# Attention of a hybrid encoder block: softmax weights and values in high and low parts, and the row maximum as a minimum of negated scores

## The chip, the cores and the metric

One core of one Trainium2 chip runs the whole block as one program. The metric is device time in microseconds (us) from the first to the last instruction of one execution, with what lies around it; lower is better. A step of 0.5% is about 7.5 us here.

## The reference, cut to what matters

The block normalizes 512 tokens of width 1024, projects them once, runs a gated mixing branch (A) and a dilated window attention (B) side by side, projects their sum back, and then does a product-key expert retrieval that takes most of the time. The change touches only branch B, whose three dilated windows the kernel merges into one masked softmax: the mask holds the logarithm of how many windows contain a pair of tokens.

```
    s = jnp.einsum('nbqhd,nbkhd->nbhqk', qb, kw).astype(jnp.float32) * (HEAD_DIM ** -0.5)
    ...
    m = jnp.max(s, axis=-1, keepdims=True)
    p = jnp.exp(s - m)
    l = jnp.sum(p, axis=-1)
    o = jnp.einsum('nbhqk,nbkhd->nbqhd', p, vw.astype(jnp.float32))
    l_t = jnp.swapaxes(l, 2, 3)
    o = o / l_t[..., None]
```

There are 8 heads of 64 columns and 4 blocks of 128 query tokens, so 32 pairs of block and head.

## The kernel before, in words

The order of instructions on each engine is the order in which they are written (a manual schedule): each engine works through its own list, and semaphores that the tile framework places hold an instruction until its operands are there and its output buffer is free. In the code T is TensorE, V is VectorE (DVE), S is ScalarE (ACT), G is GpSimd (POOL), Q is SyncE's DMA queue.

Most large products are done in two parts. `split` (lines 78 to 80) copies a float32 tensor into an fp32r tile (the high part, on ACT) and subtracts that from the source (the low part, on DVE by `sub`); a product is then three passes, high by high, high by low and low by high. The attention's second product, weights by values, is not done so before the change: it is a plain float32 product, and the trace counts two TensorE instructions for each.

The attention runs over s = 0 to 31, with i the block of queries and h the head. Its parts are staged in a loop (lines 493 to 504), which writes for each s, in this order: the exponential of s+2 (ACT, line 409), the transposes of s+1 (four on PE, line 416) and their copy out of PSUM (ACT, line 418), the scores of s+3 (two products of 512 columns on PE, lines 394 and 395), the masked maximum of s+3 (DVE, line 402) with its negation (line 404), and the product with the values of s (PE, line 429, in `att_mix`). Once in eight steps `att_out` divides a block by the sums (DVE), `att_sq` squares it (ACT), and `turn_gated` transposes a part of branch A (PE, ACT and DVE, lines 487 to 491).

Buffers: the score tiles in PSUM are two ("pu"), the transposed weights in PSUM are one ("tr"), the softmax tiles `sm` two (tag w1), their transposes `st` two (tag w2). Ahead of the loop the scores and maxima of 0, 1 and 2 are done, the exponentials of 0 and 1, the transposes of 0, and the four value tiles `vs` (lines 479 to 483), which are evicted from the projection's PSUM tiles by ACT and DVE in turn. Behind the loop comes the output projection (line 237), of which the first products need nothing of the attention.

`h2T` is a pair of tiles of 128 x 8 x 512 that hold the second layer's input later on; until then `h2T[1]` holds low parts of the keys.

Of the kernel before, what the change touches and what calls it, by code (L numbers as in the profile page):

```python
# [8 lines left out]
F32 = mybir.dt.float32  # L9
F32R = mybir.dt.float32r  # L10
# [4 lines left out]
AF = mybir.ActivationFunctionType  # L15
ALU = mybir.AluOpType
# [4 lines left out]
NB = 4  # L21
# [4 lines left out]
HD = 64  # L26
# [18 lines left out]
def peer_block(ctx: ExitStack, tc: tile.TileContext, A, out):  # L45
    nc = tc.nc
    V, S, G, T, Q = nc.vector, nc.scalar, nc.gpsimd, nc.tensor, nc.sync
# [9 lines left out]
    tk = tr_ctx.enter_context(tc.tile_pool(name="tk", bufs=1))  # L57
# [20 lines left out]
    def split(hi, lo, src, sub):  # L78
        S.copy(hi, src)  # L79
        sub.tensor_tensor(lo, src, hi.bitcast(F32), op=ALU.subtract)  # L80
# [48 lines left out]
    def inv_root(pool, ss, n, cols=1, name="sd", bias=eps):  # L129

        sd = pool.tile([128, 2, cols], F32, name=name, bufs=4 if name == "sd" else 1)
        S.activation(sd[:, 0, :], ss, AF.Sqrt, bias=bias, scale=1.0 / n)
        V.reciprocal(sd[:, 1, :], sd[:, 0, :])
        return sd[:, 1, :]
# [107 lines left out]
    def drain(gen, n=10 ** 6):  # L242
        for _ in range(n):
            if next(gen, True):
                return


    h2T = [keep.tile([128, KT, 512], F32R, name=f"h2T{i}") for i in range(2)]
    qk = {"q": [], "k": []}

# [39 lines left out]
    ps = []  # L290
# [19 lines left out]
    xrs = inv_root(tk, xss, 1024, NB, name="xrs")  # L310
# [3 lines left out]
    ps = []  # L314
# [17 lines left out]
    masks = {}  # L332
# [7 lines left out]
    ps = []  # L340
# [11 lines left out]
    va = tk.tile([128, NB, 512], F32, name="va")  # L352
# [7 lines left out]
    ps = []  # L360
# [22 lines left out]
    pss, sms, pos, sts = {}, {}, {}, {}  # L383
    l8 = tk.tile([128, NB, 2, H], F32, name="l8")
    mxs = {}

    def att_scores(s):
        if s < NS:
            i, h = divmod(s, H)
            if h == 0:  # L390
                mask_load(i + 1)
            pss[s] = pu.tile([128, 512], F32, name="pu")
            q, k, klo = qk["q"][h // 2][0][:, h % 2, i * 128:(i + 1) * 128], *qk["k"][h // 2]
            T.matmul(pss[s], q, k[:, h % 2, :], start=True, stop=False)
            T.matmul(pss[s], q, klo[:, h % 2, :], start=False, stop=True)

    def att_max(s):
        if s < NS:
            i, h = divmod(s, H)
            sms[s] = tk.tile([128, 512], F32, name="sm", tag="w1", bufs=2)  # L400
            mx = mxs[s] = tk.tile([128, 2], F32, name="mx", bufs=4)
            V.tensor_tensor_reduce(sms[s], pss.pop(s), masks[i], op0=ALU.add, op1=ALU.max, scale=HD ** -0.5,
                                   scalar=-3.0e38, accum_out=mx[:, 0:1])
            V.tensor_scalar(mx[:, 1:2], mx[:, 0:1], -1.0, None, op0=ALU.mult)

    def att_exp(s):
        if s < NS:
            i, h = divmod(s, H)
            S.activation(sms[s], sms[s], AF.Exp, bias=mxs.pop(s)[:, 1:2], accum_out=l8[:, i, 0, h:h + 1])

    def att_turn(s):
        if s < NS:
            sm = sms.pop(s)
            ps = pr.tile([128, 512], F32, name="tr")
            for j in range(NB):
                T.transpose(ps[:, j * 128:(j + 1) * 128], sm[:, j * 128:(j + 1) * 128], ident)  # L416
            sts[s] = tk.tile([128, 512], F32, name="st", tag="w2", bufs=2)
            S.copy(sts[s], ps)

    def att_mix(s):  # L420
        i, h = divmod(s, H)
        if h == 0:
            if i % 2:
                pos[i] = pr.tile([128, 512], F32, name="po")
            else:
                pos[i] = pr.tile([128, 512], F32, name="acc", bufs=4)
        st = sts.pop(s)
        for j in range(NB):
            T.matmul(pos[i][:, h * HD:(h + 1) * HD], st[:, j * 128:(j + 1) * 128], vs[:, j, h * HD:(h + 1) * HD],  # L429
                     start=(j == 0), stop=(j == NB - 1))  # L430

    msq = tk.tile([128, 2, NB], F32, name="msq")
    bo = {}
# [15 lines left out]
    ps = []  # L449
    gen = proj(16, hT, ps)  # L450
    drain(gen, 4)
    for g in range(0, 8, 2):
# [3 lines left out]
        for j in range(2):  # L456
            us = ua[:, :, (g + j) * 64:(g + j + 1) * 64]
            V.scalar_tensor_tensor(us, pm[:, j, :].rearrange("p (b c) -> p b c", b=NB), bsp[:, g + j:g + j + 1], us,
                                   op0=ALU.add, op1=ALU.mult)
        drain(gen, 1)  # L460
    for b in range(NB):
        sq = tk.tile([128, 512], F32, name="scr", tag="w3", bufs=2)
        sumsq(sq, ua[:, b, :], msq[:, 0, b:b + 1])
    att_scores(0)
    att_max(0)
    drain(gen, 2)
    urs = inv_root(tk, msq[:, 0, :], 512, NB)
    warm(AF.Exp)
    att_scores(1)
    att_max(1)  # L470
    drain(gen, 2)
    att_exp(0)
    for b in range(NB):
        V.tensor_scalar(ua[:, b, :], ua[:, b, :], urs[:, b:b + 1], None, op0=ALU.mult)
    drain(gen)
    vs = tk.tile([128, NB, 512], F32, name="vs", tag="va")
    att_exp(1)
    att_turn(0)
    for b in range(NB):
        if b % 2:  # L480
            V.tensor_scalar(vs[:, b, :], ps[b], xrs[:, b:b + 1], None, op0=ALU.mult)
        else:
            S.activation(vs[:, b, :], ps[b], AF.Copy, scale=xrs[:, b:b + 1])
    att_scores(2)
    att_max(2)

    def turn_gated(k):
# [5 lines left out]
    for s in range(NS):  # L493
        att_exp(s + 2)
        att_turn(s + 1)
        if s % H == 1 and s > H:
            att_sq(s // H - 1)
        att_scores(s + 3)
        att_max(s + 3)
        if s % H == 0 and s:  # L500
            att_out(s // H - 1)
        if s % H == 4:
            turn_gated(s // H)
        att_mix(s)
# [355 lines left out]
    for t8 in range(N8):  # L860
        a, c = hot.pop(0)
# [198 lines left out]
    for e in range(NK):  # L1060
# [16 lines left out]
        n = min(int(quota), 128 - dotted)  # L1077
# [110 lines left out]
```

## Time and profile before

| | before |
|---|---|
| median of 3 runs | 1513.45 us (1510.02 to 1516.0) |
| the profiled execution: time | 1517.74 us |
| the profiled execution: span of the trace | 1515.9 us |
| mean granted TensorE clock | 0.988 |
| PE busy, share of the span | 97% |
| DVE busy | 76% |
| ACT busy | 42% |
| POOL busy | 19% |

The profiled execution took 1.84 us more than its span, and 4.3 us more than the median of the runs. Busy shares are means over stages with different limits. The attention lies in about 60 us of the span, between 145 and 205 us.

### The profile page before, as it was taken

The numbers are of one execution on the slowest core, as the hardware profiler recorded it, in microseconds if no ns is written. First come the engines' busy times: TensorE is split into PE (matmuls) and PEld (weight loads), VectorE is DVE, ScalarE is ACT, GpSimd is POOL, SyncE is SP. The second block draws the span as 40 slices with busy tenths as digits, with TensorE's granted clock in tenths as the row PEclk, the third lists the DMA queues.
The fourth block names the chain that finished last, engine by engine and source line by source line (L and its number), as shares of the span: only waits on it lengthen the run. The fifth ranks groups of instructions, "written<-read, shape, count | busy, mean of one in ns | idle before, by whom it ended". The sixth has DMA issues, their size and how long they took to land.

```text
span 1515.9 us, 21652 instructions
## 1 busy us (share of the span) xinstructions
PE 1469.3 (97%) x7977; PEld 1302.9 (86%) x7977; DVE 1159.2 (76%) x2407; ACT 640.4 (42%) x1088; POOL 294.3 (19%) x230
## 2 busy tenths in 40 slices
PE   8899999999899999999999999999999999999997
PEld 6677988888888889789999999999999999987785
DVE  3644554789899967878888888888888888877775
ACT  5354753344455643434333333333333333333334
POOL 0242001444700000012221222222122222211002
PEclk9999999999999999999999999999999999999999
DMA  4231032333356775479999999889999999988764
GB/s 158 91 97 63 29 110 86 92 94 104 105 208 252 264 278 195 132 260 357 333 333 340 333 328 341 311 314 332 331 333 330 316 330 333 312 285 285 263 209 158
DMA packets 130073, 357.21 MB, mean 236 GB/s; under 512 B 9136, under 2 KB 62128, under 8 KB 113456
## 3 DMA queue, kind: packets, MB, share of 16 engines
q1 hardware_dynamic: 104624, 196.45, 39.5%
q0 software_dynamic: 18432, 134.23, 23.2%
q10 hardware_dynamic: 6912, 25.17, 4.1%
q8 instruction: 62, 1.02, 0.3%
q14 instruction: 43, 0.35, 0.1%
HBM read 325.40 MB, written 30.41 MB: 235 GB/s over the span
## 4 chain that ended last, share of the span: by engine, by line
PE 73%; DVE 13%; DMA 6%; issue 3%; ACT 3%; POOL 1%; ACTq 0%; SPq 0%; DVEq 0%; POOLq 0%
PE pu L187 31%; PE acc L990 27%; PE acc L237 7%; DMA vraw<-in_uv_dram 4%; DVE ohb L829 3%; DVE oha L833 2%; DVE ulo L167 2%; DMA uraw<-in_uT_dram 2%; DVE vlo L80 2%; PE tr L416 1%; ACT vhi L79 1%; PE tr L712 1%; PE pu L237 1%; PE po L429 1%; POOL ulo L167 1%
## 5 line engine op out<-in xcount | busy, mean ns | idle before, releaser
L187 PE MATMUL pu<-h2T,uhi 128*128 128x384 f32 (+2 forms) x2336 | 451.0, 343 | 3.1 <-ACT act L742 2.4
L187 PEld LDWEIGHTS pu<-h2T,uhi 128*128 128x128 f32 x2336 | 409.8, 189 | 18.9 <-ACT act L742 2.7
L936 POOL DMA_INDIRECT uv<-in_uv_dram,ei x128 | 168.1, 1313 | 847.5 <-DVE xlast L951 355.7
L80 DVE TENSOR_TENSOR vlo<-vraw,vhi 128x1024 fp32r<-128x1024 f32 x128 | 156.8, 1225 | 151.5 <-ACT vhi L79 151.5
L79 ACT CAST vhi<-vraw 128x1024 fp32r<-128x1024 f32 x128 | 134.5, 1051 | 282.0 <-issue 169.8
L990 PE MATMUL acc<-vlo,wahi 128*128 128x512 f32 x768 | 240.8, 395 | 7.8 <-DVE vlo L80 7.1
L990 PE MATMUL acc<-vhi,wahi 128*128 128x512 f32 x768 | 240.3, 394 | 2.3 <-ACT wahi L79 2.2
L990 PE MATMUL acc<-vhi,walo 128*128 128x512 f32 x768 | 239.3, 393 | 0.0
L187 PE MATMUL pu<-h2T,ulo 128*128 128x384 f32 (+2 forms) x1168 | 235.3, 341 | 2.0 <-POOL ulo L167 2.0
L187 PEld LDWEIGHTS pu<-h2T,ulo 128*128 128x128 f32 x1168 | 205.1, 189 | 6.8 <-POOL ulo L167 2.3
L156 ACT CAST uhi<-uraw 128x1024 fp32r<-128x1024 f32 x144 | 150.7, 1047 | 75.6 <-DMA uraw<-in_uT_dram 62.2
L990 PEld LDWEIGHTS acc<-vlo,wahi 128*128 128x128 f32 x768 | 144.5, 189 | 43.3 <-DVE vlo L80 12.1
L990 PEld LDWEIGHTS acc<-vhi,walo 128*128 128x128 f32 x768 | 144.6, 189 | 32.2 <-DVE walo L80 1.4
L951 DVE SCALAR_TENSOR_TENSOR xlast<-uv,dot,xlast 128x1024 f32<-128x1024 f32 x128 | 164.5, 1285 | 4.5
L990 PEld LDWEIGHTS acc<-vhi,wahi 128*128 128x128 f32 x768 | 143.3, 189 | 28.2 <-ACT wahi L79 4.4
L167 DVE TENSOR_TENSOR ulo<-uraw,uhi 128x1024 fp32r<-128x1024 f32 x116 | 141.6, 1221 | 29.4 <-ACT uhi L156 29.3
L942 DVE SCALAR_TENSOR_TENSOR uv<-uv,h 128x1024 f32<-128x1024 f32 x128 | 153.8, 1219 | 8.0 <-DMA uv<-in_uv_dram,ei 8.0
L742 ACT ACTIVATE act<-pu 128x384 f32<-128x384 f32 x128 | 62.9, 491 | 223.1 <-PE pu L187 222.7
L167 POOL TENSOR_TENSOR ulo<-uraw,uhi 128x512 fp32r<-128x512 f32 x56 | 81.4, 1477 | 209.5 <-ACT uhi L156 209.5
L79 ACT CAST wahi<-wa 128x384 fp32r<-128x384 f32 x128 | 65.3, 510 | 28.5 <-DVE wa L975 28.2
L975 DVE TENSOR_TENSOR wa<-act,wt 128x384 f32<-128x384 f32 x128 | 70.6, 552 | 1.8 <-DMA wt<-wd 1.8
L80 DVE TENSOR_TENSOR walo<-wa,wahi 128x384 fp32r<-128x384 f32 x128 | 70.7, 553 | 0.6 <-ACT wahi L79 0.6
(249 smaller groups left out, 1507.3 us busy)
## 6 DMA issues: line engine op xcount, KB each, us to landing
uraw<-in_uT_dram SPq DMA_DIRECT2D x128, 512.0 KB, 5.9
vraw<-in_uv_dram SPq DMA_DIRECT2D x128, 512.0 KB, 5.4
wd<-wst ACTq DMA_DIRECT2D x48, 512.0 KB, 3.3
wt<-wd SPq DMA_DIRECT2D x32, 768.0 KB, 11.0
wraw<-in_w_in_dram SPq DMA_DIRECT2D x19, 512.0 KB, 3.7
uraw<-in_w_q_dram SPq DMA_DIRECT2D x16, 512.0 KB, 3.9
wraw<-in_w_out_dram SPq DMA_DIRECT2D x4, 512.0 KB, 3.9
wrawq<-in_w_out_dram SPq DMA_DIRECT2D x4, 512.0 KB, 5.8
```

Of the source, the lines that this page charges most:

```text
L79: S.copy(hi, src)
L80: sub.tensor_tensor(lo, src, hi.bitcast(F32), op=ALU.subtract)
L156: S.copy(hi, raws[i])
L167: eng.tensor_tensor(lo[:, k, :], raws[i][:, k, :], hi[:, k, :].bitcast(F32), op=ALU.subtract)
L187: T.matmul(o, l[:, k, :], r[:, k, t0:n], start=(p == 0 and k == 0), stop=(p == 2 and k == KT - 1))
L237: T.matmul(out[b], l[:, b * 128:(b + 1) * 128], r[:, kk, :], start=(k == 0 and i == 0), stop=(k == KT - 1 and i == 2))
L742: S.activation(acts[e], o[:, :DT], AF.Gelu_apprx_tanh)
L936: G.indirect_dma_start(out=uvs[r].rearrange("p s d -> p (s d)"), out_offset=None, in_=A["uv"], in_offset=bass.IndirectOffsetOnAxis(ap=ei[: ...
L942: V.scalar_tensor_tensor(uv[:, 0, :], uv[:, 0, :], 1.0, h2, op0=ALU.mult, op1=ALU.mult, accum_out=d[:, 0:1])
L951: V.scalar_tensor_tensor(xlast, uv[:, 1, :], d[:, 1:2], xlast, op0=ALU.mult, op1=ALU.add)
L975: eng.tensor_tensor(wa.rearrange("p (c t) -> p c t", c=NWC), acts.pop(e).rearrange("p (c t) -> p c t", c=NWC), wts[e // WG][:, :, e % WG, ...
L990: T.matmul(acc[b][n], l[:, c], r[:, n * 512:(n + 1) * 512], start=(e == 0 and i == 0), stop=(e == NK - 1 and i == 2))
```

## The change: what it does

- The maximum: the tensor-tensor reduction now scales by the negated factor and reduces with a minimum, so what it leaves is the bias that the exponential needs; the separate negation of the 128 x 1 maximum is gone, and the exponential reads the negated scores with a scale of -1.
- The transposed weights: `split` takes the place of the copy. ACT writes the high part to `st`, DVE then subtracts it from the same PSUM tile and writes the low part to a row of `h2T[0]`.
- The values: ACT evicts all four high parts, DVE makes the four low parts, which lie in the first four rows of `h2T[0]`.
- The product with the values: for each 128 keys three fp32r products of 64 columns in place of one float32 product of 64 columns.

```diff
-            mx = mxs[s] = tk.tile([128, 2], F32, name="mx", bufs=4)
-            V.tensor_tensor_reduce(sms[s], pss.pop(s), masks[i], op0=ALU.add, op1=ALU.max, scale=HD ** -0.5,
-                                   scalar=-3.0e38, accum_out=mx[:, 0:1])
-            V.tensor_scalar(mx[:, 1:2], mx[:, 0:1], -1.0, None, op0=ALU.mult)
+            mx = mxs[s] = tk.tile([128, 1], F32, name="mx", bufs=4)
+            V.tensor_tensor_reduce(sms[s], pss.pop(s), masks[i], op0=ALU.add, op1=ALU.min, scale=-HD ** -0.5,
+                                   scalar=3.0e38, accum_out=mx)
...
-            S.activation(sms[s], sms[s], AF.Exp, bias=mxs.pop(s)[:, 1:2], accum_out=l8[:, i, 0, h:h + 1])
+            S.activation(sms[s], sms[s], AF.Exp, bias=mxs.pop(s), scale=-1.0, accum_out=l8[:, i, 0, h:h + 1])
...
-            sts[s] = tk.tile([128, 512], F32, name="st", tag="w2", bufs=2)
-            S.copy(sts[s], ps)
+            sts[s] = (tk.tile([128, 512], F32R, name="st", tag="w2", bufs=2), h2T[0][:, 4 + s % 2, :])
+            split(*sts[s], ps, V)
...
-        st = sts.pop(s)
+        shi, slo = sts.pop(s)
         for j in range(NB):
-            T.matmul(pos[i][:, h * HD:(h + 1) * HD], st[:, j * 128:(j + 1) * 128], vs[:, j, h * HD:(h + 1) * HD],
-                     start=(j == 0), stop=(j == NB - 1))
+            c = slice(j * 128, (j + 1) * 128)
+            for n, (l, r) in enumerate(((shi, vhi), (shi, vlo), (slo, vhi))):
+                T.matmul(pos[i][:, h * HD:(h + 1) * HD], l[:, c], r[:, j, h * HD:(h + 1) * HD],
+                         start=(j == 0 and n == 0), stop=(j == NB - 1 and n == 2))
...
-    vs = tk.tile([128, NB, 512], F32, name="vs", tag="va")
+    vhi, vlo = tk.tile([128, NB, 512], F32R, name="vs", tag="va"), h2T[0][:, 0:NB, :]
     att_exp(1)
     att_turn(0)
     for b in range(NB):
-        if b % 2:
-            V.tensor_scalar(vs[:, b, :], ps[b], xrs[:, b:b + 1], None, op0=ALU.mult)
-        else:
-            S.activation(vs[:, b, :], ps[b], AF.Copy, scale=xrs[:, b:b + 1])
+        S.activation(vhi[:, b, :], ps[b], AF.Copy, scale=xrs[:, b:b + 1])
+        V.scalar_tensor_tensor(vlo[:, b, :], ps[b], xrs[:, b:b + 1], vhi[:, b, :].bitcast(F32), op0=ALU.mult,
+                               op1=ALU.subtract)
```

## Rows read from the trace of the kernel before

**Rows 1.** The page, part 1: busy time, share and instructions of each engine.

```profile
PE 1469.3 (97%) x7977; PEld 1302.9 (86%) x7977; DVE 1159.2 (76%) x2407; ACT 640.4 (42%) x1088; POOL 294.3 (19%) x230
```

**Rows 2.** Busy time by stretch: the attention, and a pause before it.

```profile
76.00:78.00 2.00, 0.00 (x0) 0.00 (x0) 0.83 (x1) 0.00 (x0) 1.95 (x1) 0.73 0.07 7
78.00:80.00 2.00, 2.00 (x6) 1.61 (x7) 0.68 (x1) 0.73 (x2) 0.73 (x2) 0.50 0.82 245
...
145.00:205.00 60.00, 59.41 (x466) 55.71 (x465) 32.64 (x104) 44.40 (x104) 0.00 (x0) 1.00 0.06 19
```

**Rows 3.** The chain of waits, one step of the attention: start, length, what.

```profile
172.19 0.23 PE pu L394
172.42 0.24 PE pu L395
172.65 0.84 PE po L429 x8
173.49 0.44 PE tr L416 x4
```

**Rows 4.** Groups of instructions from 148 to 204 us.

```profile
L409 ACT ACTIVATE sm<-sm,mx 128x512 f32<-128x512 f32 x30 | 21.7, 722 | 12.1 <-DVE mx L404 12.1
L402 DVE CUSTOM_DVE_ANT_0 sm<-pu,mask 128x512 f32<-128x512 f32 x29 | 20.1, 692 | 22.0 <-ACT sm L409 11.3 <-PE pu L395 10.6
```

**Rows 5.** The timeline, ACT and DVE in one step of the loop.

```profile
171.59 0.72 ACT L409 ACTIVATE sm<-sm,mx 128x512 f32<-128x512 f32 x1
...
172.32 0.56 ACT L418 COPY st<-tr 128x512 f32<-128x512 f32 x1
...
172.69 0.69 DVE L402 CUSTOM_DVE_ANT_0 sm<-pu,mask 128x512 f32<-128x512 f32 x1 [0.21 <-PE pu L395]
...
173.31 0.08 DVE L402 DVE_READ_ACCUMULATOR2_ANT mx<- 128x1 f32 x1
...
173.43 0.15 DVE L404 TENSOR_SCALAR mx<-mx 128x1 f32<-128x1 f32 x1
...
173.67 0.72 ACT L409 ACTIVATE sm<-sm,mx 128x512 f32<-128x512 f32 x1 [0.79 <-DVE mx L404]
```

**Rows 6.** The timeline ahead of the loop.

```profile
146.34 0.58 ACT L418 COPY st<-tr 128x512 f32<-128x512 f32 x1 [4.03 <-PE tr L416]
...
146.82 1.27 ACT L483 ACTIVATE vs<-acc,xrs 128x512 f32<-128x512 f32 x2
...
147.97 0.73 ACT L409 ACTIVATE sm<-sm,mx 128x512 f32<-128x512 f32 x1
```

**Rows 7.** The timeline at the loop's end.

```profile
200.99 0.72 ACT L409 ACTIVATE sm<-sm,mx 128x512 f32<-128x512 f32 x1
...
204.63 0.48 PE L237 MATMUL acc<-wph,thi 128*128 128x512 f32 x1
```

**Rows 8.** The timeline behind the attention: `split` of a 128x512 PSUM tile.

```profile
260.36 0.58 ACT L79 CAST h2T<-tr 128x512 fp32r<-128x512 f32 x1 [4.33 <-PE tr L568]
...
260.97 0.69 DVE L80 TENSOR_TENSOR h2T<-tr,h2T 128x512 fp32r<-128x512 f32 x1 [3.06 <-ACT h2T L79]
...
261.58 0.68 DVE L80 TENSOR_TENSOR h2T<-po,h2T 128x512 fp32r<-128x512 f32 x1
```

**Rows 9.** The chain of waits: 48 fp32r passes of 256 columns, 8 float32 passes of 128.

```profile
254.13 5.75 PE pu L187 x48
...
267.02 0.89 PE tr L712 x8
```

**Rows 10.** The timeline of DVE: low parts made with a scale.

```profile
217.31 1.41 DVE L198 SCALAR_TENSOR_TENSOR tlo<-pu,gains,thi 128x512 fp32r<-128x512 f32 x2 [4.36 <-ACT thi L197]
218.63 0.74 DVE L198 SCALAR_TENSOR_TENSOR tlo<-tr,gains,thi 128x512 fp32r<-128x512 f32 x1
```

**Rows 11.** The timeline where products read `h2T` while other columns are written.

```profile
253.89 2.15 PE L187 MATMUL pu<-h2T,uhi 128*128 128x256 f32 x16
...
254.97 0.57 ACT L79 CAST h2T<-tr 128x512 fp32r<-128x512 f32 x1
```

## The prediction

> **What bounds the kernel now.** The page comes first: PE is busy 97% of the span [rows 1], so as a whole the kernel is bound by TensorE. The change lies in one stage only, so the table by stretches is read next. In the 60 us of the attention PE is busy 59.41 us, ACT 44.40, DVE 32.64, and the granted clock is 1.00, its upper level of 2.4 GHz [rows 2]. So PE sets the pace there too, and ACT comes second. The chain of waits confirms it: one step is 0.23 + 0.24 us of scores, 0.84 us for the eight passes of the product with the values, and 0.44 us of four transposes, 1.75 us in all, and nothing but PE is on it [rows 3]. The groups of that stretch show what the other two do: DVE's maximum and ACT's exponential both stand idle before they start, 22.0 us and 12.1 us in total, and wait for each other or for PE [rows 4]. That idle time costs nothing as long as PE is full, but it tells that DVE and ACT hand work to each other in every step. The timeline of one step gives the hand-overs [rows 5], and the first and last exponential of the loop give its pace: exponential 2 starts at 147.97 [rows 6], exponential 31 at 200.99 [rows 7], so 29 steps in 53.02 us, 1.83 us each (1.75 plus the occasional transposes of branch A and some small waits).
>
> **The change part by part.** *A new loop between ACT and DVE.* What matters most is not a price but an order. In each step ACT has to do exponential s+2 and then the high part of s+1. DVE has to do the low part of s+1, which needs that high part, and then the maximum of s+3. Exponential s+3 then needs this maximum. Each engine goes through its list in the order written, as the rows show for the parts that are there now (exponential, copy, exponential on ACT). So four instructions follow one another, and the next step's first needs this step's last. Before the change there was no such ring: the copy had no user on DVE, and the maximum did not stand behind it. The length of the ring is worked out from the rows:
>
> - exponential to the next ACT instruction, start to start: 171.59 to 172.32, 0.73 us [rows 5];
> - high part to low part: the same `split` of a 128x512 PSUM tile stands behind the attention, 260.36 to 260.97, 0.61 us [rows 8];
> - low part to the next DVE instruction: 260.97 to 261.58, 0.61 us [rows 8];
> - maximum to exponential: 172.69 to 173.31 for the reduction, 0.08 us to read the accumulator, and a hand-over of 0.09 us, which is what lies between the end of the negation (173.43 + 0.15) and 173.67 [rows 5]; together 0.79 us. The 0.15 us of the negation and its gap are gone and not counted.
>
> The ring takes 2.74 us. Below, with the shortest overlap that these rows allow, I take 2.65; above, with whole durations and a hand-over of 0.1 us at each of the three crossings that the change leaves, 2.95. The minimum in place of the maximum and the scale of -1 I cost at nothing: instruction and shape are the same.
>
> *PE in one step.* Twelve fp32r passes of 64 columns take the place of eight float32 passes. The trace has no fp32r pass of 64 columns. From above: one of 256 columns takes 5.75 / 48 = 0.120 us [rows 9], and fewer columns can't take longer. From below: by columns alone a quarter of that, 0.03 us. I take 0.105 us, the 0.84 / 8 of today's 64-column passes [rows 3], since a float32 pass of 128 columns takes only 0.89 / 8 = 0.111 us [rows 9]: halving the columns took nearly nothing away, so something other than columns, the load of 128 weights for each pass, seems to set it. Then PE needs 0.47 + 0.44 + 12 x 0.105 = 2.17 us a step (1.27 to 2.35 at the ends), which is under 2.74 at every end. PE is no longer the bound, and the price of a pass drops out of the sum.
>
> *The single transpose buffer.* Transposes s+2 have to wait until the low part s+1 has been read out of "tr", which comes 0.68 us after it starts; 0.45 us of transposes end about 1.2 us after that start. High part s+2 can start only at 0.61 + 0.79 + 0.73 = 2.13 us. So this wait is covered by 0.9 us. The work of one step in eight is covered as well: the division on DVE (about 0.9 us) and branch A's low part fit into the 1.3 us in which DVE waits for ACT, and the squares on ACT into the 1.4 us in which ACT waits for DVE.
>
> *Ahead of the loop.* High part 0 starts at 146.34 as now [rows 6], low part 0 at 146.95, free at 147.56. Then DVE makes four low parts of the values at 0.66 us each (two in 1.41 us, the third 1.32 us after the first [rows 10]), so maximum 2, which is written behind them, starts at 150.20 and exponential 2 at 150.99, in place of 147.97: +3.0 us. ACT's four evictions, 0.58 us apart (two in 1.27 us [rows 6]), run ahead of DVE and cost nothing more.
>
> *In the loop.* 29 x 2.74 = 79.5 us in place of 53.0: +26.4 us.
>
> *Behind the loop.* From exponential 31 to the output projection it is 3.64 us now [rows 7]. After the change: 0.73 to high part 30, 0.61 to its low part, 0.73 until transposes 31 may start, 0.45 for them, 0.05 + 0.61 to low part 31, 0.73, and 1.26 us of products: 5.17 us, +1.5 us.
>
> *The clock.* In the new prologue PE has about 2.2 us of work between 146.4 and 153 us, since the product of step 0 waits for the last low part of the values and transposes 2 for low part 1. The trace shows what a pause can do: PE stands still from 76 to 78 us, and in the next two microseconds the granted clock is 0.50, the lower level of 1.2 GHz [rows 2]. At that level a PE step would take up to 4.3 us instead of 2.17 and overrun the ring by 1.6 us a step for some two steps. I take 1 us, between 0 and 4.
>
> The sum is 26.4 + 3.0 + 1.5 + 1 = +32 us. Against the profiled execution's 1517.74 us that makes 1550; its time is 4.3 us above the median of the runs, so for the median I take 1513.45 + 32 = 1545.5 us. Everything behind the attention starts that much later, and no load that limits it is issued early enough to gain from that. The bounds of the ring (-2.6, +6.1) and of the clock (-1, +3) give 1541.5 to 1555 for this case.
>
> A rule of the Trainium skill speaks against all this. Its page "TensorE: Matmul & The Clock Gate", section "Back-to-back issue gap", gives some 60 cycles for an isolated matmul of 1 to 64 columns. By that, as an estimate from that page, a pass would take 0.025 us and twelve of them 0.3 us. The 0.105 us of rows 3 for each 64-column pass in this very loop speak against it, since it already has far fewer columns than time.
>
> **The rivals.**
>
> *PE stays the bound.* If the two engines overlap as freely as now, the step is PE's 2.17 us in place of 1.75: 0.42 x 32 = +13.4 us, 1527 us. For it: ACT and DVE have idle time in plenty [rows 4]. Against it: that idle time is no slack once each waits for the other in turn. Chance 0.05.
>
> *Fewer passes' worth of time, faster.* If a 64-column fp32r pass costs its columns alone, 0.03 us, the product takes 0.36 us in place of 0.84, and PE's step 1.27. ACT's exponential and high part, 0.73 + about 0.5, would then set the pace at about 1.3 us: 0.53 x 29 = 15 us less, 2 us lost ahead of the loop, 1500 us. It decides only if the ring is shorter than 1.83 us, and its four bare durations alone (0.72, 0.58, 0.68, 0.69) make 2.67. Chance 0.03, with the 60-cycle rule in it.
>
> *The tracking of `h2T[0]` is coarse.* Low parts of weights and values are rows of one tile. If writes and reads of different rows held each other, the product of step s would wait for low part s+1, and transposes and high part s+2 for that product: 0.68 + 0.05 + 1.26 + 0.5 = 2.5 us in place of 2.13, a ring of 3.15 and +12 us more, 1557 us. Against it: products that read columns 0 to 255 of `h2T` start at 253.89, while ACT writes other columns of it at 254.97 [rows 11]. Chance 0.04.
>
> *The clock stays low.* PE would be busy 2.17 / 2.74 = 79% of a step. If that does not hold the clock up and it stays at 1.2 GHz, the step is PE's 4.3 us: (4.3 - 2.74) x 29 = +45 us more, 1590 us; half of the time, 1568. Chance 0.06.
>
> **How the numbers follow.** The forecast has the remaining 0.82. Its own range of 1541.5 to 1555 leaves out too much beside unknown costs, so the range reaches down toward the PE-bound case and up past the coarse one: 1535 to 1562. No measurement of this kernel tells less than 0.5% (7.5 us) from no change. Faster: the second rival, 0.03. Same: the space between it and the first, 0.02. Slower: the rest, 0.95.
>
> **What would show it.** Exponentials 2.7 us apart in the loop; DVE's low part waiting for ACT's high part in nearly every step, and ACT's exponential waiting for DVE's maximum; PE about 80% busy between 146 and 236 us, its transposes waiting for DVE; the product of step s still about 0.1 us a pass; the output projection starting near 236 instead of 204.63. The prediction is wrong if exponentials stand 2.2 us or less apart, if DVE takes the maximum before the low part, or if the clock's row falls under 1.00 for most of the stage.

## The result, and the profile after

The changed kernel takes 1557.22 us (median of 6 runs, 1552.61 to 1564.09), the kernel before 1515.86 us (6 runs, 1510.02 to 1517.85): a ratio of 1.0282, with a 95% interval of 1.0263 to 1.0301. It is slower by 41 us, where 32 were forecast; the time lies inside the range of 1535 to 1562, and 2 us above the narrower 1541.5 to 1555 that the forecast's own terms gave.

The profiled execution has a span of 1556.3 us, 40.4 more than before, and a mean granted clock of 0.982. The timeline of ACT, DVE and PE in one step of the loop, where [rows 5] stood before:

```profile
194.65 0.69 DVE L80 TENSOR_TENSOR h2T<-tr,st 128x512 fp32r<-128x512 f32 x1 [1.41 <-ACT st L79]
...
195.26 0.68 DVE L403 CUSTOM_DVE_ANT_0 sm<-pu,mask 128x512 f32<-128x512 f32 x1
...
195.87 0.08 DVE L403 DVE_READ_ACCUMULATOR2_ANT mx<- 128x1 f32 x1
...
196.04 0.72 ACT L409 ACTIVATE sm<-sm,mx 128x512 f32<-128x512 f32 x1 [1.43 <-DVE mx L403]
...
196.77 0.56 ACT L79 CAST st<-tr 128x512 fp32r<-128x512 f32 x1
...
197.36 0.69 DVE L80 TENSOR_TENSOR h2T<-tr,st 128x512 fp32r<-128x512 f32 x1 [1.41 <-ACT st L79]
...
198.11 0.66 PE L416 MATMUL tr<-ident,sm 128*128 128x128 f32 x4 [0.33 <-DVE h2T L80]
```

Low part, maximum, exponential, high part, and the next low part: 0.61 + 0.78 + 0.73 + 0.59 = 2.71 us, and every link starts within 0.1 us of the end of the one before it. DVE and ACT stand still for 1.4 us in turn. PE, which was full in [rows 3], now waits for DVE before its transposes. The chain of waits shows the same ring in place of PE:

```profile
231.27 0.07 ACT sm L409
231.34 0.56 issue
231.90 0.19 ACT sm L409
232.09 0.48 ACT st L79
...
232.59 0.62 DVE h2T L80
233.21 0.67 DVE sm L403
233.88 0.02 DVE mx L403
```

The groups from 148 to 236 us, beside [rows 4]: ACT's wait for the maximum has grown from 12.1 to 38.3 us, DVE's low part waits 42.3 us for ACT, and the maximum waits for nobody, because it always comes straight behind the low part.

```profile
L409 ACT ACTIVATE sm<-sm,mx 128x512 f32<-128x512 f32 x30 | 21.7, 723 | 38.3 <-DVE mx L403 38.3
L416 PE MATMUL tr<-ident,sm 128*128 128x128 f32 x116 | 20.9, 307 | 9.0 <-DVE h2T L80 9.0
L80 DVE TENSOR_TENSOR h2T<-tr,st 128x512 fp32r<-128x512 f32 x30 | 20.8, 692 | 42.3 <-ACT st L79 42.3
L403 DVE CUSTOM_DVE_ANT_0 sm<-pu,mask 128x512 f32<-128x512 f32 x30 | 20.4, 681 | 0.0
```

That is not all. The exponentials on ACT's timeline, first ahead of the loop and in it:

```profile
149.76 0.72 ACT L409 ACTIVATE sm<-sm,mx 128x512 f32<-128x512 f32 x1 [1.74 <-DVE mx L403]
152.47 0.72 ACT L409 ACTIVATE sm<-sm,mx 128x512 f32<-128x512 f32 x1 [1.43 <-DVE mx L403]
155.18 0.72 ACT L409 ACTIVATE sm<-sm,mx 128x512 f32<-128x512 f32 x1 [1.43 <-DVE mx L403]
159.22 0.72 ACT L409 ACTIVATE sm<-sm,mx 128x512 f32<-128x512 f32 x1 [1.42 <-DVE mx L403]
163.40 0.72 ACT L409 ACTIVATE sm<-sm,mx 128x512 f32<-128x512 f32 x1 [1.43 <-DVE mx L403]
...
233.98 0.72 ACT L409 ACTIVATE sm<-sm,mx 128x512 f32<-128x512 f32 x1 [0.84 <-DVE mx L403]
```

Two steps are 2.71 us, then come four of 3.6 to 4.4. The table by stretches says why (length, busy time of PE, PEld, DVE, ACT and POOL, granted clock, DMA); the line under it is from PE's timeline:

```profile
147.00:150.50 3.50, 2.25 (x16) 1.83 (x14) 2.67 (x6) 1.76 (x5) 0.00 (x0) 1.00 0.00 0
150.50:154.00 3.50, 2.18 (x9) 1.98 (x9) 1.51 (x4) 1.83 (x5) 0.00 (x0) 0.53 0.02 5
154.00:158.00 4.00, 4.00 (x19) 3.81 (x19) 1.25 (x4) 1.40 (x3) 0.00 (x0) 0.50 0.00 0
...
166.00:170.00 4.00, 4.00 (x28) 3.77 (x26) 2.06 (x5) 2.13 (x5) 0.00 (x0) 0.78 0.18 63
...
182.00:236.00 54.00, 47.75 (x369) 44.00 (x366) 29.06 (x67) 28.72 (x67) 0.00 (x0) 1.00 0.05 16
...
236.00:240.00 4.00, 3.95 (x19) 3.96 (x20) 0.80 (x2) 0.58 (x1) 0.00 (x0) 0.50 0.00 0
```

```profile
151.82 1.11 PE L416 MATMUL tr<-ident,sm 128*128 128x128 f32 x4 [2.30 <-DVE h2T L80]
```

PE is 64% busy ahead of the loop and then stands still for 2.3 us; in that pause the clock falls to 1.2 GHz. It stays there for about 17 us, in which PE, once it has work again, is full and sets the step. It falls a second time at the loop's end, behind a pause of 0.8 us, for about 10 us, into the output projection.

The 40.4 us, stretch by stretch: up to the first transposes -1.2 (the first of two slow spells early in the kernel, in work that the change does not touch, lasted 3.4 us in place of 6.8); from there to exponential 2, 5.3 us in place of 2.3, +3.0; the loop to exponential 31, 84.2 us in place of 53.0, +31.2; from there to the output projection at 241.9 us, 8.0 in place of 3.6 [rows 7], +4.3; the rest +3.1. The loop's 31.2 are 25.6 of ring (29 x 2.71 against 53.0) and 5.6 of slow clock, of which 0.3 is one longer step with a division. Of the 7.4 behind it, 1.5 are the ring's tail as forecast, and about 5 the second slow spell: its four transposes take 1.1 us, not 0.66, its passes are 0.21 us apart, not 0.11, and the first 48 products of the projection take 13.25 us where they took 11.29.

### The profile page after: what moved, and what is told of

Same layout as the page of the kernel before. It is cut to its first block, busy times and chain, and to the rows that moved or that the text cites. A ratio compares the mean times of both kernels' runs of the same rounds, so it can differ in the third digit from the quotient of the medians.

```text
span 1556.3 us, 21910 instructions
## 1 busy us (share of the span) xinstructions
PE 1497.0 (96%) x8105; PEld 1326.4 (85%) x8105; DVE 1175.4 (76%) x2409; ACT 641.6 (41%) x1090; POOL 294.3 (19%) x230
## 4 chain that ended last, share of the span: by engine, by line
PE 70%; DVE 15%; DMA 6%; issue 4%; ACT 4%; POOL 1%; ACTq 0%; SPq 0%; DVEq 0%; POOLq 0%
PE pu L187 29%; PE acc L991 27%; PE acc L237 7%; DMA vraw<-in_uv_dram 4%; DVE ohb L830 3%; DVE oha L834 2%; DVE ulo L167 2%; DMA uraw<-in_uT_dram 2%; DVE vlo L80 1%; DVE sm L403 1%; PE pu L237 1%; PE tr L713 1%; ACT vhi L79 1%; ACT st L79 1%; PE acc L431 1%
```

## The experiments

Theory: a ring of four instructions on ACT and DVE sets the step, and slow spells of TensorE's clock, which begin where PE has to pause, add about 10 us. Rivals: that PE's twelve passes in place of eight are the cost, and that the slow spells are harmless or come of themselves. "Step" is the distance of exponentials at the upper clock (for fused_spread the mean over the loop); the clock is that of the profiled execution.

| run | step, us | mean clock | median, us | ratio to before, interval |
|---|---|---|---|---|
| changed kernel | 2.71 | 0.982 | 1557.22 | 1.0282, 1.0263 to 1.0301 |
| ring_plain | 2.71 | 0.990 | 1545.71 | 1.0205, 1.0186 to 1.0224 |
| stale_low | 2.22 | 0.987 | 1538.29 | 1.0161, 1.0142 to 1.0179 |
| max_first | 2.58 | 0.983 | 1549.57 | 1.0217, 1.0196 to 1.0237 |
| filler | 2.71 | 0.990 | 1546.09 | 1.0213, 1.0183 to 1.0243 |
| min_only | as before | 0.991 | 1513.03 | 0.9985, 0.9976 to 0.9994 |
| keep_negate | 2.90 | 0.956 | 1588.63 | 1.0503, 1.0476 to 1.0530 |
| max_first_two_tr | none | 0.955 | 1591.03 | 1.0507, 1.0489 to 1.0525 |
| two_tr_filler | 2.22 | 0.992 | 1532.83 | 1.0107, 1.0091 to 1.0123 |
| fused | 1.77 | 0.963 | 1548.65 | 1.0216, 1.0193 to 1.0239 |
| fused_filler | 1.77 | 0.974 | 1536.72 | 1.0139, 1.0096 to 1.0182 |
| fused_spread | 1.84 | 0.988 | 1519.55 | 1.0021, 1.0008 to 1.0033 |

A twelfth run, keep_negate_filler, has no single figure and is told below.

**ring_plain: the ring without the passes.** The product and the values of before, the low part made and not used.

```diff
-            split(*sts[s], ps, V)
+            S.copy(sts[s], ps)
+            V.tensor_tensor(h2T[0][:, 4 + s % 2, :], ps, sts[s], op=ALU.subtract)
...
-            for n, (l, r) in enumerate(((shi, vhi), (shi, vlo), (slo, vhi))):
+            T.matmul(pos[i][:, h * HD:(h + 1) * HD], st[:, j * 128:(j + 1) * 128], vs[:, j, h * HD:(h + 1) * HD],
+                     start=(j == 0), stop=(j == NB - 1))
```

> Edit: the changed kernel with the product and the values of before (eight float32 passes), while the low part of the weights is still made by DVE in each step and not used. Theory (the ring): the step stays at 2.71 us though PE needs only 1.75 us; only the 3 us ahead of the loop go back, so about 1550 to 1556 us, with PE still emptier and the clock perhaps low for longer. Rival (the passes on PE are the cost): back to the time of before, 1516 to 1518 us.

The stretch of 182 to 200 us of its table, and two exponentials:

```profile
182.00:200.00 18.00, 13.17 (x96) 11.71 (x96) 10.55 (x24) 9.25 (x23) 0.00 (x0) 1.00 0.14 44
```

```profile
199.96 0.72 ACT L409 ACTIVATE sm<-sm,mx 128x512 f32<-128x512 f32 x1 [1.42 <-DVE mx L403]
202.66 0.72 ACT L409 ACTIVATE sm<-sm,mx 128x512 f32<-128x512 f32 x1 [1.42 <-DVE mx L403]
```

With eight passes and PE only 73% busy the step is 2.71 us all the same. The rival of the passes is out. The time is below what was expected because its slow spell lasted 7 us and not 17, and none came at the loop's end. One more thing shows here. PE stood still for 0.75 us in most steps:

```profile
215.56 0.66 PE L416 MATMUL tr<-ident,sm 128*128 128x128 f32 x4 [0.75 <-DVE h2T L419]
```

The clock was 1.00 from 157 us on all the same, also behind a pause of 1.2 us at the loop's end. So a pause of PE does not always bring the clock down.

**stale_low: the passes without the ring.** The output misses the true low part of the weights.

```diff
-            split(*sts[s], ps, V)
+            if s < 2:
+                split(*sts[s], ps, V)
+            else:
+                S.copy(sts[s][0], ps)
```

> Edit: the low part of the weights is made only for the first two steps and then left as it is, so the output misses it; the twelve passes stay. Theory (the ring): without the low part on DVE there is no ring, the step is PE's 2.17 us plus the occasional transposes, so 0.42 x 29 = 12 us in the loop and 3 us ahead of it over the kernel before, 1529 to 1535 us, with little slow clock left. Rival (the passes on PE are the cost): nothing changes on PE, 1557 us.

```profile
192.17 0.72 ACT L409 ACTIVATE sm<-sm,mx 128x512 f32<-128x512 f32 x1 [0.67 <-DVE mx L403]
194.39 0.72 ACT L409 ACTIVATE sm<-sm,mx 128x512 f32<-128x512 f32 x1 [0.68 <-DVE mx L403]
```

The step is 2.22 us, PE's own, and PE is full. A slow spell of 17 us ahead of and in the loop was still there, so the time is 3 us above the range expected. Both runs together: the low part's place between high part and maximum made the step 2.71; the four more passes made 0.4 us a step, which the ring had hidden.

**max_first: the same work, the maximum ahead of the low part.**

```diff
-            split(*sts[s], ps, V)
+            S.copy(sts[s][0], ps)
...
         att_max(s + 3)
+        att_low(s + 1)
```

> Edit: DVE takes the maximum of s+3 before the low part of s+1; all work stays. Theory (a ring of exponential, high part, low part and maximum sets the step, 2.71 us in the changed kernel, and two spells of slow clock add about 10 us): the low part drops out of the ring, the step becomes PE's 2.17 us plus a short wait for the single transpose buffer, about 2.3 us, so 29 x 0.4 = 12 us less and shorter slow spells: 1536 to 1546 us. Rival (the twelve passes in place of eight on PE are the cost): PE's work is the same, so 1557 us.

The step is 2.58 us, not 2.3, and the time lies 4 us above the range expected. The chain of waits shows what the expectation had missed:

```profile
198.06 0.61 DVE h2T L425
198.67 0.14 issue
198.81 0.63 PE tr L416 x4
199.43 0.23 PE pu L395
199.67 0.25 PE pu L396
...
200.56 0.08 DVE mx L403
200.64 0.60 DVE h2T L425
```

A second ring has closed, through the single PSUM tile "tr": the transposes wait for the low part that reads it, the scores stand behind the transposes on PE, the maximum needs the scores, and the next low part stands behind the maximum. One of its four runs took 1589.5 us, at a mean clock of 0.951.

**filler: PE kept busy where it paused.** Products of 512 columns that nobody reads: four behind the scores of 2, eight ahead of the transposes of 2, and two each in steps 29 and 30.

```diff
     att_scores(2)
+    fill(4, spare)
...
+        if s == 1:
+            fill(8, spare)
...
+        if s in (NS - 3, NS - 2):
+            fill(2, pu.tile([128, 512], F32, name="pu"))
```

> Edit: products of 512 columns that nobody reads fill the pauses of PE: four after the scores of 2, eight ahead of the transposes of 2, and two in each of the steps 29 and 30, where there are no scores left. Theory (the slow spells come from PE's pauses there and cost about 10 us of the 41): the clock stays at 2.4 GHz through the attention, steps are all about 2.71 us, and the time falls by 7 to 10 us to 1547 to 1550 us. Rival (the spells are hidden behind the ring, or come whatever PE does): no change or up to 2 us slower, 1557 to 1559 us.

```profile
151.00:182.00 31.00, 27.38 (x206) 24.80 (x204) 15.74 (x36) 16.26 (x39) 0.00 (x0) 1.00 0.03 10
182.00:230.00 48.00, 43.50 (x326) 40.12 (x326) 26.18 (x59) 24.97 (x59) 0.00 (x0) 0.96 0.06 18
```

More work on PE made the kernel 11 us faster. Both spells are gone; a new one of 3.4 us came at 182 us, behind a pause of 0.6 us that did no harm in the changed kernel. The time is 30.9 us above the kernel before, which is the forecast's sum without its clock term (26.4 + 3.0 + 1.5 = 30.9); that it fits to the tenth, with a slow spell still inside, is chance.

**min_only: the first part of the change alone, in the kernel before.**

```diff
...
-            V.tensor_scalar(mx[:, 1:2], mx[:, 0:1], -1.0, None, op0=ALU.mult)
...
```

> Edit: the kernel before with the first part of the change alone (minimum of negated scores, no negation on DVE, a scale of -1 in the exponential). Theory (before the change PE sets the step, and the exponential's 12.1 us of waiting for the negation cost nothing): no change within 0.3%, 1512 to 1518 us. Rival (that waiting is on the path): 29 x 0.19 = 5.5 us faster, 1510 us.

It is faster by 0.15%, 2.3 us, the interval just free of no change. How much of it the edit made is open: in the profiled executions the loop, exponential 2 to 31, takes 52.2 us in place of 53.0, so 0.8 us lie there, and 1.1 us were gained ahead of anything that the edit touches, where an early slow spell lasted 3.4 us in place of 6.8. It is the only version here that beats both kernels.

**keep_negate: the split without the first part.**

```diff
-            V.tensor_tensor_reduce(sms[s], pss.pop(s), masks[i], op0=ALU.add, op1=ALU.min, scale=-HD ** -0.5,
-                                   scalar=3.0e38, accum_out=mx)
+            V.tensor_tensor_reduce(sms[s], pss.pop(s), masks[i], op0=ALU.add, op1=ALU.max, scale=HD ** -0.5,
+                                   scalar=-3.0e38, accum_out=mx[:, 0:1])
+            V.tensor_scalar(mx[:, 1:2], mx[:, 0:1], -1.0, None, op0=ALU.mult)
...
```

> Edit: the changed kernel with the maximum and its negation as before; the split and the twelve passes stay. Theory (maximum and exponential are links of the ring): the negation and its gap, 0.19 us, come back into every step, 2.90 in place of 2.71 us, 29 x 0.19 = 5.5 us more, 1561 to 1564 us. Rival (the negation lies beside other work, as before the change): 1557 us.

```profile
150.83 0.72 ACT L410 ACTIVATE sm<-sm,mx 128x512 f32<-128x512 f32 x1 [1.92 <-DVE mx L405]
153.73 0.72 ACT L410 ACTIVATE sm<-sm,mx 128x512 f32<-128x512 f32 x1 [1.61 <-DVE mx L405]
```

Steps at the upper clock are 2.90 us, as the ring asks. But the time missed its range by 25 us: after the first spell the clock fell again, at about 186 us, and stayed down for 92 us, with steps of 4.2 us. With the filling products beside it (keep_negate_filler):

> Edit: the changed kernel with the maximum and its negation as before and the filling products (so it stands beside the run with filling products alone, 1546 us). Theory (maximum and exponential are links of the ring): each step is 2.90 in place of 2.71 us, 29 x 0.19 = 5.5 us more than that run, 1549 to 1554 us, if the clock holds. Rival (the 41 us over it of the run without filling products was the negation itself): near 1588 us.

Its four runs took 1552.4, 1581.9, 1582.4 and 1590.1 us at mean clocks of 0.985, 0.963, 0.962 and 0.954. The one whose clock held lies in the range; in the profiled one it fell at about 155 us in spite of the filling, where PE's pauses were 0.6 us at most, and stayed down for 126 us. So the filling did not help in three of four runs, and that the negation adds just 5.5 us rests on the steps of 2.90 us and on one run.

**max_first_two_tr: the second ring opened as well.** As max_first, with two PSUM tiles for the transposes; the product's outputs go to "acc" in turn.

```diff
-            ps = pr.tile([128, 512], F32, name="tr")
+            ps = pr.tile([128, 512], F32, name=("tr", "po")[s % 2])
...
```

> Edit: the maximum ahead of the low part, and two PSUM tiles for the transposes, so that the transposes of s+2 need not wait for the low part of s+1. Theory (with the maximum first a second ring stays, low part to transposes to scores to maximum to low part through the single PSUM tile, 2.58 us in that run; with two tiles it opens): the step is PE's 2.2 us, 0.4 us under the run with one tile, 1534 to 1540 us, about what the run without the low part gave. Rival (DVE and ACT are too busy with the low part in any order): no change against the run with one tile, 1549 us.

```profile
148.40:150.00 1.60, 0.69 (x3) 0.69 (x4) 0.80 (x3) 1.56 (x4) 0.00 (x0) 0.71 0.00 0
170.00:250.00 80.00, 80.00 (x346) 76.11 (x347) 26.72 (x61) 28.65 (x63) 0.00 (x0) 0.50 0.03 11
250.00:270.00 20.00, 20.00 (x96) 19.12 (x95) 8.06 (x18) 7.68 (x18) 0.00 (x0) 0.54 0.00 1
270.00:290.00 20.00, 20.00 (x114) 17.18 (x114) 9.50 (x16) 8.85 (x14) 0.00 (x0) 1.00 0.24 74
```

The worst run of all: the clock falls in the pause ahead of the loop, and although PE is then 100% busy it stays at 1.2 GHz for 119 us, through all but the last steps of the loop; it rises at 268.6 us, among the loop's own passes of 64 columns, 5.6 us ahead of the output projection's first product. With the filling products (two_tr_filler):

> Edit: the run with the maximum first and two transpose tiles, with products that nobody reads in PE's pauses ahead of the loop (four and eight of 512 columns) and two in each of the steps 29 and 30. Without them that run took 1591 us, with the clock at its lower level from 149 us until the output projection and steps of 4.2 us. Theory (the order of work had opened the rings, and the whole loss was the clock, which fell in the pause ahead of the loop and did not come back): the clock stays at 2.4 GHz, steps are PE's 2.2 us, 1528 to 1534 us. Rival (this loop's PE work does not hold the clock up even without a pause): it falls somewhere in the loop and the time stays above 1560 us.

```profile
150.00:212.00 62.00, 62.00 (x501) 59.08 (x499) 39.82 (x91) 42.38 (x93) 0.00 (x0) 1.00 0.06 19
```

58 us less, by twelve products in a pause and four at the end: clock 1.00 throughout, steps of 2.22 us, a time inside the range. So the order of work had opened both rings, and the clock alone had hidden it.

**fused: eight passes in place of twelve.** High and low parts of the values lie side by side, so that one pass of 128 columns does two of 64; DVE adds the halves in `att_out`.

```diff
+            T.matmul(o, shi[:, c], vv[:, j, h * 128:(h + 1) * 128], start=(j == 0), stop=False)
+            T.matmul(o[:, :64], slo[:, c], vv[:, j, h * 128:h * 128 + 64], start=False, stop=(j == NB - 1))
...
```

> Edit: as the run with two transpose tiles, and high and low parts of the values lie side by side, so that one pass of 128 columns takes the place of the two passes by the high part of the weights: 8 passes a head in place of 12; the two halves are added on DVE once in a block. Theory (a pass costs its 128 weights, about 0.11 us, for 64 as for 128 columns, and PE sets the step once the rings are open): PE's step is 0.47 + 0.44 + 8 x 0.11 = 1.79 us, the pace of the kernel before; with 3 us ahead of the loop, the additions and a slow spell there, 1520 to 1528 us. Rival (passes cost their columns): 4 x 128 + 4 x 64 columns are as many as 12 x 64, no change against the run with two tiles, 1534 to 1540 us.

```profile
168.26 0.22 PE L435 MATMUL acc<-h2T,st 128*128 128x128 f32 x1
168.32 0.24 PE L436 MATMUL acc<-h2T,slo 128*128 128x64 f32 x1
...
169.07 0.65 PE L416 MATMUL tr<-ident,sm 128*128 128x128 f32 x4
...
177.04 0.30 PE L436 MATMUL acc<-h2T,slo 128*128 128x64 f32 x1 [1.50 <-DVE slo L425]
```

```profile
189.00:250.00 61.00, 61.00 (x256) 57.07 (x255) 29.47 (x70) 27.11 (x58) 0.00 (x0) 0.50 0.00 1
```

Eight passes take 0.81 us, 0.10 each on average, and the step is 1.77 us, though the columns are as many as in twelve passes of 64: the number of passes sets the price here, not their columns. But the time missed its range by 21 us. At 175 us PE waited 1.5 us for a low part that stood on DVE behind the seven instructions of `att_out` and a maximum; the clock fell behind that pause, at 179 us, and PE, 100% busy from 189 us on, had 0.50 until 250 us. The filling products alone (fused_filler) did not prevent that:

> Edit: the run with high and low parts of the values side by side, 8 passes a head, with the same filling products. Theory (a pass costs its 128 weights, not its columns; at the upper clock the run without filler had steps of 1.77 us): steps of 1.8 us throughout, the pace of the kernel before, so 3 us ahead of the loop and 1 to 2 us for additions and filling products remain, 1517 to 1523 us. Rival (the clock falls all the same in PE's full loop, as it did in the middle of the run without filler, at 179 us): 1540 to 1550 us as there.

Its runs took 1529.95 to 1546.89 us, the longer the lower their mean clock; in the profiled one the clock fell twice, each time behind a pause of 1.5 us of the same kind. fused_spread then took the pause away: half a block is divided at a time, and its additions go to GpSimd.

> Edit: as the run of the side-by-side values with filling products, but the division by the sums is done for half a block at a time, four heads each, and its additions go to GpSimd; the squares come one step later. In the runs before, six DVE instructions in a row at each eighth step held up the low part, PE waited 1.5 us for it, and the clock fell behind that pause. Theory (this pause, in a loop that cannot bring the clock back, was what was lost): the clock stays at 2.4 GHz, steps are 1.8 us throughout, 1517 to 1523 us, the time of the kernel before within 0.5%. Rival (the loop with 8 passes lets the clock fall anyhow): 1530 to 1550 us with much spread, as there.

```profile
150.00:170.00 20.00, 20.00 (x158) 18.70 (x157) 16.34 (x39) 15.13 (x36) 1.45 (x2) 1.00 0.04 14
170.00:205.00 35.00, 35.00 (x277) 32.67 (x276) 29.73 (x73) 26.83 (x63) 2.92 (x4) 1.00 0.07 24
```

PE full, clock 1.00, and the three-part product at 1.0021 of the time of the plain one.

## Why the prediction held, and where it did not

*The number.* That the time lies in the range owes something to the range: the forecast's own, 1541.5 to 1555, missed it by 2 us and had been widened for unknown costs. Of the 11.7 us between 1545.5 and 1557.2, 2.4 are the kernel before, whose median of 3 runs was 1513.45 us and of 6 is 1515.86; nearly all the rest is the clock, below.

*The ring* was forecast at 2.74 us and is 2.71, link by link. ring_plain and stale_low show that it and not PE set the step, and keep_negate's 2.90 that maximum and exponential are links of it.

*Ahead of the loop* +3.0 forecast, +3.0 measured. *Behind it* +1.5 forecast; +4.3 measured, the excess being slow clock.

*PE's price.* Taken at 0.105 us a pass, measured 0.11 in the changed kernel. It did drop out of the sum at the upper clock; stale_low and two_tr_filler show the 2.2 us that lay under the ring. The 60 cycles (0.025 us as an estimate) that the Trainium skill's page "TensorE: Matmul & The Clock Gate" gives in its section "Back-to-back issue gap" for an isolated matmul of so few columns do not describe these passes, which each load new weights; the measured 0.11 us decides.

*The covered waits* (the transposes through "tr", the occasional work) stayed covered at the upper clock but for one step of 2.99 us; ACT waited for transposes in four cases only, all in the slow spell.

*The coarse tracking* of `h2T[0]` had been put at 1557 us, which is where the time came out; that is chance. Its ring of 3.15 us did not come, and PE's product waited for a low part on DVE only twice, 0.5 us in all, ahead of the loop.

*The clock* is the step that failed in its size: 1 us was taken, with 4 at most, and it cost about 10 (5.6 in the loop, about 3 at its end, 2 in the projection), and filler took 11 back. The place and the mechanism were named, but the length was guessed at two steps, where the spell lasted 17 us (and two steps of 1.6 us would have made 3 us by the prediction's own working, not 1), and the thinner work at the loop's end was not seen as a second such place. The rival "the clock stays low", given 0.06, did not come in the changed kernel's six runs, but the clock stayed low for 44 to 126 us in five of its near relatives (keep_negate, keep_negate_filler, max_first_two_tr, fused, fused_filler).

*The negation* was costed as a part of the ring, which held. That the kernel before measured 0.15% faster without it was not foreseen; it lies under the 0.5% that was called measurable, and 0.8 of its 2.3 us are all that a pair of traces shows in the loop.

What stays open: why the clock came back after 17 us in the changed kernel, stale_low and max_first, and only after 72 to 126 us in keep_negate, keep_negate_filler, max_first_two_tr and fused, with PE full in all of them; and why pauses of 0.5 to 0.8 us went ahead of a fall in some runs and not in ring_plain. The filling products put work of 512 columns where PE had paused, so no run here separates the pause from the kind of work around it.

## What to carry to other kernels

Where two engines work through fixed lists, follow every step's hand-overs around: an instruction put between two others on one engine can close a ring whose length is the sum of its links, however idle both engines look, and opening it may uncover the next ring through a single buffer. Price a pause of PE by what follows it, not by its own length: a pause of one or two microseconds cost 5 to 58 us here. Sixteen useless products took that back in filler and two_tr_filler, but not in three of four runs of keep_negate_filler, so check the clock's row afterwards. And where each pass loads its own 128 weights, count passes and not columns: two thin products with one stationary side belong into one pass.

## What the hardware showed that was not expected

A PE that is 100% busy does not by itself get the upper clock back. In max_first_two_tr the clock was 0.50 from 149.0 to 268.6 us, with PE full from 150 us on, and it rose in the loop's last steps with the passes of 64 columns still running; in two_tr_filler the very same loop, entered without a pause, ran at 1.00 for 62 us. So this loop can keep either level; which of them it had in these two runs hung on what PE did before it. It can also bring the upper level back: in the changed kernel, with the same passes, the clock was up again after 17 us. Nor does a pause by itself bring the clock down: ring_plain's PE, 73% busy with a pause of 0.75 us in most steps, kept 1.00 from 157 us on.
